# Transposing the heads' results by transfers instead of on TensorE, and taking the last norm's mean off by matmuls

## The chip, the cores and the metric

The kernel runs on one core of one Trainium2 chip. The metric is the time of one execution on the device in microseconds; three plain runs of the kernel before took 1237.16, 1237.46 and 1241.87 us, median 1237.46.

The engines are named as in the profile: PE (TensorE, matmuls; PEld its weight loads), DVE (VectorE), ACT (ScalarE), POOL (GpSimd), SP (SyncE, which issues most transfers). Each runs its own instructions in order and waits on semaphores for the others. SBUF is the memory that all engines and transfers use, PSUM holds the banks that TensorE accumulates into.

## The reference

A decoder trunk of two layers over 256 tokens of width 1024, all in float32. Each layer is

```
x <- LN(alpha*x + 0.5*SwiGLU_1(x))       # width 2816
x <- LN(alpha*x + Mixer(x))
x <- LN(alpha*x + 0.5*SwiGLU_2(x))
```

The mixer projects x to `u, v, q, k, val` and two gates. Branch A norms `gelu(v)`, mixes it over positions by a masked 128x128 matrix in each of 8 channel groups, and multiplies by `gelu(u)`. Branch B is a differential attention with 8 heads: two softmaxes of 64-wide halves of q and k are subtracted, the result is applied to a 128-wide value, and each head's 128 numbers of a token are divided by their root mean square (the part that this change touches):

```
o = a @ v                                    # per head, 256 tokens x 128
o = o * rsqrt(mean(o*o) + eps) * g * (1 - lambda_init)
m = sigmoid(gA) * (h_A @ W_A) + sigmoid(gB) * (h_B @ W_B);  out = m @ W_out
```

## The kernel before

TensorE multiplies in a fast float32 form, and accuracy comes from splitting every operand in a coarse part ("hi") and the rest ("lo"): three products stand for one. Weights are streamed. `stream` loads a piece of 128 x 2048 float32 into one of four "raw" buffers (L154, on SP's queue); ScalarE writes the coarse half pieces `whi` (L167) and VectorE the rest `wlo` (L169) into eight buffers each, so that TensorE works several pieces behind the loads.

Two loops do the large products. `gemm_a2` makes outputs transposed (channels on partitions, the 256 tokens along the row): for each source two blocks of 128 channels, each with eight matmuls of 512 columns (L221, tokens' hi and lo side by side) and eight of 256 (L228). Then ScalarE copies one half of the bank out (L229) and VectorE adds the other (L231), which frees the bank. There are four banks for this, two for a source, so a bank is needed again two sources later. `gemm_b` and `gemm_b2` make outputs with tokens on partitions (L209).

The order of TensorE's instructions is the order in which the program writes them. What is small runs beside the large loops as tasks: a generator is resumed when the count of "beats" (blocks of large matmuls; one source of `gemm_a2` is two beats) has gone on by what it last yielded. On the other engines a scheduler sorts by priority and by what can be ready, and `behind(ins)` puts an instruction after another one of its engine without a wait for it.

In the mixer the sources come as val, then q and k of four head pairs (called hp0 to hp3 here), eight sources of the two gates, v, u, and the two branches. Attention of a head pair is a task (`attend`) that starts when its q and k are there and so runs over the next pairs' projections and over the gates. Its end: TensorE makes `on`, 128 tokens x (2 token halves x 2 heads x 128); ScalarE copies it (L643) and sums squares (L648); GpSimd computes the reciprocal root in fifteen small steps (L651, then `rsqrt4`, L194 to L202); ScalarE rescales `on` (L657); TensorE transposes it in four 128x128 matmuls into a side bank (L662); ScalarE and VectorE split it into `hb` (L667, L668), which the branch reads much later.

The feed-forward part already has a transposition by transfers, for four of its blocks: float32 numbers are seen as pairs of 16-bit words; GpSimd copies them into two planes of words (L498), SP issues one transposing transfer for each plane (L502), and GpSimd joins the planes again (L505).

The norms are made with tokens on partitions. The last one (`last=True`) ends the kernel: statistics in groups (L414, L419), mean off and times g in three pieces (L433), reciprocal root from ScalarE's square root with one Newton step on VectorE (L435 to L437), times root plus b in three pieces (L439), each sent out when ready (L441).

Of the kernel before, what the change touches and what calls it, by code (L numbers as in the profile page):

```python
# [11 lines left out]
F32 = mybir.dt.float32  # L12
# [3 lines left out]
U16 = mybir.dt.uint16  # L16
# [35 lines left out]
def trunk(ctx, tc, x, xT, w13a, w13b, w2, wb, wqk, wa, wbr, wo, gateb, sgug, sgub, sguwT, sgubias, lam, diffg,  # L52
# [89 lines left out]
    latest, added, emptied, silu, turned_by, loaded = [None, None], [None], [None], [None], [None], [None]  # L142
# [5 lines left out]
    def stream(src, width=CH, sub=HC, lent=(), after=(None, None)):  # L148
# [22 lines left out]
        return out  # L171

# [208 lines left out]
    def bc_load(src, after):  # L381
        t = res.tile([P, D], F32, tag="bc", name=name("bc"), bufs=2)
        V.tensor_copy(t[:, :1], after)  # L383
        G.dma_start(t, src.partition_broadcast(P))  # L384
        return t

    class Norm:

# [3 lines left out]
        def __init__(self, l, i, scale, eps, after, last=False):  # L392
# [7 lines left out]
            if last:  # L400
                A.activation(self.g, self.g, AF.Copy, scale=-0.5)
                with behind(silu[0]):
                    A.activation(sm("first", 1), mask[:, :1], AF.Sqrt)
            else:
                self.x = [xs.tile([P, 4, 512], F32R, tag="x", name=name("x")) for _ in range(2)]

        def part(self, t, c, ps):
# [4 lines left out]
            for o in range(s.start, s.stop, self.group):  # L412
                g = o // self.group * 6
                V.bn_stats(out=self.st[t][:, g : g + 6], in_=self.y[t][:, o : o + self.group])  # L414

        def finish(self, t, waits):
# [10 lines left out]
            cuts = (0, 512, 768, D)  # L427
            cuts = [slice(*c) for c in zip(cuts, cuts[1:])]
            ve, sd, r, a = (sm(n, 1) for n in ("ve", "nwy", "nwa", "nwy"))
            V.tensor_scalar(out=ve, in0=mv[:, 1:2], scalar1=self.eps, scalar2=None, op0=ALU.add)  # L430
            A.activation(sd, ve, AF.Sqrt)
            for s in cuts:
# [5 lines left out]
            for n, s in enumerate(cuts):  # L438
                V.scalar_tensor_tensor(out=y[:, s], in0=y[:, s], scalar=r, in1=self.b[:, s],  # L439
                                       op0=ALU.mult, op1=ALU.add)  # L440
                (nc.sync, A)[n % 2].dma_start(out[t * P : (t + 1) * P, s], y[:, s])  # L441
# [37 lines left out]
    def ffn(l, f, i, norm, last=False):  # L479
# [5 lines left out]
        def front(t, ps):  # L485
# [4 lines left out]
            beside(turned(t, p), 0)  # L490

        def turned(t, p):


            pairs = [p[:, n].bitcast(U16).rearrange("p (c w) -> p w c", w=2) for n in range(2)]
            there, back = (p[:, n].bitcast(U16).rearrange("p (w c) -> p w c", w=2) for n in range(2))
            for w in range(2):
                G.tensor_copy(out=there[:, w], in_=pairs[1][:, w])  # L498
            yield 17
            with behind(loaded[0]):  # L500
                for w in range(2):
                    nc.sync.dma_start(back[:, w].rearrange("p (k t) -> p k t", k=4), there[:, w], transpose=True)  # L502
            yield 6
            for w in range(2):
                G.tensor_copy(out=pairs[0][:, w], in_=back[:, w])  # L505
# [33 lines left out]
    def mixer(l, i, norm):  # L539
# [34 lines left out]
        def attend(hp, qT, kT):  # L574
# [83 lines left out]
            yield 0.9  # L658
            b = side_bank()
            for j in range(2):  # L660
                for t in range(NT):
                    PE.transpose(b[:, j * T + t * P : j * T + (t + 1) * P], on[:, (t * 2 + j) * P : (t * 2 + j + 1) * P],  # L662
                                  ident)
            dl = dgs[:, l : l + 1]
            for j in range(2):
                h, s = hb[hp * 2 + j], slice(j * T, (j + 1) * T)
                A.activation(h[:, :T], b[:, s], AF.Copy, scale=dl)  # L667
                V.scalar_tensor_tensor(out=h[:, T:], in0=b[:, s], scalar=dl, in1=h[:, :T].bitcast(F32),  # L668
                                        op0=ALU.mult, op1=ALU.subtract)
# [36 lines left out]
        for h in range(2):  # L706
            s = slice(h * 512, h * 512 + 512)
            G.dma_start(wsT[h], sguwT[l][:, s])
# [142 lines left out]
```

## Time and profile before

| what | value |
|---|---|
| plain runs, median of 3 | 1237.46 us |
| profiled execution | 1238.15 us, span 1236.4 us |
| granted TensorE clock | 0.998 |
| busy: PE / DVE / ACT / POOL | 1226.6 / 883.1 / 754.3 / 133.7 us |
| transposes of the heads' results (L662) | 32 matmuls, 4.8 us busy, first at 272.2, last at 925.7 us |
| transposing transfers (L502) | 16, all in the feed-forward parts |
| attention's end in the first mixer | rescaling of hp0 to hp3 at 271.0, 286.2, 298.9, 311.7 us |
| last large matmul to last output transfer | 1228.0 to 1233.7 us |

A row of the timeline has the start in us, the time it took (for several merged instructions from the first's start to the last's end), the engine, the line in the kernel, the operation, the tiles out<-in, their shape and how many; in brackets the idle time before and what ended it. A row by line gives the shortest, median and longest duration in ns. Idle time of an engine that nothing waits for costs nothing.

### The profile page before, as it was taken

How to read it: one execution, taken by the hardware profiler on the slowest of the kernel's cores; microseconds unless marked ns; L12 is line 12 of the kernel's file. 1: busy time of each engine (PE TensorE's matmuls, PEld its weight loads, DVE VectorE, ACT ScalarE, POOL GpSimd, SP SyncE). 2: the span in 40 equal slices, each digit the busy share in tenths (PEclk: the TensorE clock that was granted, in tenths of full speed). 3: DMA queues.
4: the chain of work that ended last, by engine and by line, in shares of the span. 5: the costliest groups of instructions: out<-in, count | busy, mean ns of one | idle time of the engine just before them, and what ended most of it. 6: DMA issues, size and time to landing. Idle time of an engine off the chain costs nothing.

```text
span 1236.4 us, 17873 instructions
## 1 busy us (share of the span) xinstructions
PE 1226.6 (99%) x6663; PEld 1059.8 (86%) x6663; DVE 883.1 (71%) x1533; ACT 754.3 (61%) x1386; POOL 133.7 (11%) x214
## 2 busy tenths in 40 slices
PE   9999999999999999999999999999999999999997
PEld 8888888888888888888888888888888888888886
DVE  6777567887587987665676765679866879866753
ACT  7676446679665566664466664466885654766640
POOL 1200000244100021000021000002440000210000
PEclk9999999999999999999999999999999999999999
DMA  9965645654754747557547546556456456555540
GB/s 345 265 243 188 222 174 187 223 176 161 257 180 143 244 154 236 180 175 255 195 162 224 186 158 250 204 182 219 168 175 231 151 178 230 196 196 204 177 164 35
DMA packets 49383, 243.97 MB, mean 197 GB/s; under 512 B 14048, under 2 KB 15120, under 8 KB 23184
## 3 DMA queue, kind: packets, MB, share of 16 engines
q1 hardware_dynamic: 45328, 230.18, 54.0%
q0 software_dynamic: 3536, 12.13, 3.3%
q8 instruction: 52, 0.85, 0.3%
q10 hardware_dynamic: 432, 0.52, 0.1%
q14 instruction: 35, 0.29, 0.1%
HBM read 235.47 MB, written 1.05 MB: 191 GB/s over the span
## 4 chain that ended last, share of the span: by engine, by line
PE 97%; ACT 1%; DVE 1%; issue 0%; DMA 0%; SPq 0%; POOL 0%; DVEq 0%; POOLq 0%; ACTq 0%
PE bank L221 37%; PE bank L209 35%; PE bank L228 19%; PE bank L324 2%; PE sbank L588 1%; PE sbank L460 1%; PE sbank L721 1%; PE sbank L640 1%; ACT pp L602 0%; PE sbank L336 0%; PE sbank L638 0%; PE sbank L662 0%; PE sbank L625 0%; DMA swap<-z 0%; DVE qk L568 0%
## 5 line engine op out<-in xcount | busy, mean ns | idle before, releaser
L169 DVE TENSOR_TENSOR wlo<-raw,whi 128x1024 fp32r<-128x1024 f32 (+1 forms) x442 | 498.2, 1145 | 230.8 <-PE bank L228 122.3
L167 ACT ACTIVATE whi<-raw 128x1024 fp32r<-128x1024 f32 (+1 forms) x442 | 425.5, 978 | 280.8 <-PE bank L209 135.3
L221 PE MATMUL bank<-x,whi 128*128 128x512 f32 x1792 | 425.0, 391 | 0.0
L221 PEld LDWEIGHTS bank<-x,whi 128*128 128x128 f32 x1792 | 330.9, 188 | 66.3
L228 PE MATMUL bank<-x,wlo 128*128 128x256 f32 x1792 | 230.9, 284 | 0.0
L228 PEld LDWEIGHTS bank<-x,wlo 128*128 128x128 f32 x1792 | 225.6, 191 | 5.7
L209 PE MATMUL bank<-whi,hhi 128*128 128x512 f32 (+1 forms) x374 | 141.2, 378 | 0.0
L209 PE MATMUL bank<-wlo,hhi 128*128 128x512 f32 (+1 forms) x374 | 141.0, 377 | 0.0
L209 PE MATMUL bank<-whi,hlo 128*128 128x512 f32 (+1 forms) x374 | 140.9, 377 | 0.0
L229 ACT ACTIVATE r<-bank 128x256 f32<-128x256 f32 x256 | 96.6, 379 | 66.4 <-PE bank L228 66.1
L209 PE MATMUL bank<-whi,x 128*128 128x512 f32 x328 | 105.7, 392 | 0.0
L209 PEld LDWEIGHTS bank<-whi,hlo 128*128 128x128 f32 x374 | 70.4, 188 | 13.0
L209 PEld LDWEIGHTS bank<-wlo,hhi 128*128 128x128 f32 x374 | 70.4, 188 | 12.7
L209 PEld LDWEIGHTS bank<-whi,hhi 128*128 128x128 f32 x374 | 70.4, 188 | 12.7
L209 PEld LDWEIGHTS bank<-whi,x 128*128 128x128 f32 x328 | 61.6, 188 | 12.6
L209 PE MATMUL bank<-wlo,x 128*128 128x512 f32 x164 | 63.9, 390 | 0.0
L384 POOL DMA_DIRECT2D bc<-in_lng x6 | 3.2, 534 | 480.2 <-DVE bc L383 480.2
L466 ACT ACTIVATE xf<-sbank,ln_b,ln_g 128x128 f32<-128x128 f32 x80 | 30.1, 457 | 40.1 <-PE sbank L460 40.1
L231 DVE TENSOR_TENSOR silu<-bank,r 128x256 f32<-128x256 f32 x144 | 54.2, 416 | 0.5 <-ACT r L229 0.5
L564 POOL TENSOR_TENSOR swap<-swap,sin_t 128x512 f32<-128x512 f32 x16 | 26.6, 1664 | 244.1 <-DMA swap<-z 239.3
L410 DVE SCALAR_TENSOR_TENSOR xtok<-xtok,bank 128x512 f32<-128x512 f32 (+1 forms) x25 | 16.5, 662 | 42.7 <-PE bank L209 42.7
L498 POOL COPY planes<-planes 128x512 uint16<-128x512 uint16 x16 | 27.1, 1718 | 177.4 <-DVE planes L489 177.4
(174 smaller groups left out, 1295.6 us busy)
## 6 DMA issues: line engine op xcount, KB each, us to landing
raw<-in_w13a SPq DMA_DIRECT2D x72, 1024.0 KB, 5.0
raw<-in_w SPq DMA_DIRECT2D x40, 1024.0 KB, 4.9
raw<-in_wa SPq DMA_DIRECT2D x24, 1024.0 KB, 6.0
raw<-in_wb SPq DMA_DIRECT2D x16, 1024.0 KB, 5.0
raw<-in_wqk SPq DMA_DIRECT2D x16, 1024.0 KB, 5.2
raw<-in_wbr SPq DMA_DIRECT2D x16, 1024.0 KB, 4.9
raw<-in_w13b SPq DMA_DIRECT2D x12, 1024.0 KB, 5.1
raw<-in_wo SPq DMA_DIRECT2D x8, 1024.0 KB, 5.0
```

The costliest lines, as they stand in the source:

```text
L167: A.activation(h, r, AF.Copy)
L169: V.tensor_tensor(out=w, in0=r, in1=h.bitcast(F32), op=ALU.subtract)
L209: PE.matmul(ps, xx, w, start=start and n == 0, stop=stop and n == 2)
L221: PE.matmul(b[-1], hi[:, k * P : (k + 1) * P], xc(k), start=k == 0, stop=False)
L228: PE.matmul(b[n][:, :T], lo[:, k * P : (k + 1) * P], xc(k)[:, :T], start=False, stop=k == KT - 1)
L229: emptied[0] = A.activation(r[:, s], b[n][:, T:], AF.Copy, scale=scale).ins
L231: a = V.tensor_tensor(out=z[:, s], in0=b[n][:, :T], in1=r[:, s], op=ALU.add)
L324: PE.matmul(ps[t][m], x[:, j, o + t * P : o + (t + 1) * P], y, start=k0 + j == 0 and o == 0 and y is hi, stop=k0 + j == KT - 1 and y is lo)
L410: V.scalar_tensor_tensor(out=self.y[t][:, s], in0=self.y[t][:, s], scalar=self.scale, in1=ps, op0=ALU.mult, op1=ALU.add)
L466: A.activation(xf[:, s], b[:, s], AF.Identity, scale=self.gT[:, f], bias=self.bT[:, f])
L498: G.tensor_copy(out=there[:, w], in_=pairs[1][:, w])
L564: turned_by[0] = G.tensor_tensor(out=s3, in0=s3, in1=s, op=ALU.mult).ins
```

## The change

Three edits.

1. The transposition by transfers becomes a function, `transposed`, and the heads' results use it too: GpSimd makes the planes in a new buffer `moved`, SP transposes them into `on`, GpSimd joins them in `moved`, and the split into `hb` reads `moved`. The waits between are counted in beats: 1 after the rescaling, 10 before the transfers are placed in SP's queue, then 0.3 and 0.3. The 32 TensorE transposes are gone. The split instructions are placed behind the last emptying of a bank.
2. In the last norm the second token half's first 768 columns are multiplied by g as soon as their statistics are taken. For two of the three pieces TensorE then adds, in a side bank, identity times y and a diagonal of minus the mean times g; ScalarE makes that diagonal from the negative identity. The pieces go in the opposite order, the small ones first. Variance plus epsilon is made on GpSimd, and ScalarE's square root takes epsilon as its bias from the raw variance.
3. The spatial weights' load on GpSimd's queue is placed behind the latest broadcast load (`spread`).

```diff
+    def transposed(src, out, via, first, second):
+        def planes(v):
+            return v.bitcast(U16).rearrange("p (w c) -> p w c", w=2)
+        def numbers(v):
+            return v.bitcast(U16).rearrange("p (c w) -> p w c", w=2)
+        for w in range(2):
+            G.tensor_copy(out=planes(out)[:, w], in_=numbers(src)[:, w])
+        yield first
+        with behind(loaded[0]):
+            for w in range(2):
+                nc.sync.dma_start(planes(via)[:, w].rearrange("p (k t) -> p k t", k=4), planes(out)[:, w],
+                                  transpose=True)
+        yield second
+        for w in range(2):
+            G.tensor_copy(out=numbers(out)[:, w], in_=planes(via)[:, w])
...
-        G.dma_start(t, src.partition_broadcast(P))
+        spread[0] = G.dma_start(t, src.partition_broadcast(P)).ins
...
+                self.minus = s512("minus")
+                A.activation(self.minus[:, :P], ident, AF.Copy, scale=-1.0)
...
+            if self.last and t == NT - 1 and s.stop < D:
+                V.tensor_tensor(out=self.y[t][:, s], in0=self.y[t][:, s], in1=self.g[:, s], op=ALU.mult)
...
-            V.tensor_scalar(out=ve, in0=mv[:, 1:2], scalar1=self.eps, scalar2=None, op0=ALU.add)
-            A.activation(sd, ve, AF.Sqrt)
-            for s in cuts:
+            G.tensor_scalar(out=ve, in0=mv[:, 1:2], scalar1=self.eps, scalar2=None, op0=ALU.add)
+            A.activation(sd, mv[:, 1:2], AF.Sqrt, bias=self.eps_t)
+            rows = [y[:, s] for s in cuts]
+            if t == NT - 1:
+                rows[1:] = [side_bank()[:, : s.stop - s.start] for s in cuts[1:]]
+                for b, s in zip(rows[1:], cuts[1:]):
+                    PE.matmul(b, ident, y[:, s], start=True, stop=False)
+                diag = self.minus[:, P : 2 * P]
+                A.activation(diag, self.minus[:, :P], AF.Copy, scale=mv[:, 0:1])
+                for b, s in zip(rows[1:], cuts[1:]):
+                    PE.matmul(b, diag, self.g[:, s], start=False, stop=True)
+            for s in cuts[: 1 if t == NT - 1 else 3]:
...
-            yield 0.9
-            b = side_bank()
-            for j in range(2):
-                for t in range(NT):
-                    PE.transpose(b[:, j * T + t * P : j * T + (t + 1) * P], on[:, (t * 2 + j) * P : (t * 2 + j + 1) * P],
-                                  ident)
+            yield 1
+            moved = slots("moved", 2)[0]
+            yield from transposed(on, moved, on, 10, 0.3)
+            yield 0.3
...
+                with behind(emptied[0]):
+                    A.activation(hi, f, AF.Copy, scale=dl)
+                with behind(added[0]):
+                    V.scalar_tensor_tensor(out=lo, in0=f, scalar=dl, in1=hi.bitcast(F32), op0=ALU.mult,
+                                            op1=ALU.subtract)
...
-            G.dma_start(wsT[h], sguwT[l][:, s])
+            with behind(spread[0]):
+                G.dma_start(wsT[h], sguwT[l][:, s])
```

The order on GpSimd in the first mixer, at the start of hp2's root (`ss` is its sum of squares; `ve`, `yi`, `nwa`, `nwy` its steps). Lines are those of each kernel: L651 and L194 to L202 before are L675 and L215 to L223 now. Before:

```order
L202 TENSOR_TENSOR nwy_2860<-nwa_2859,nwy_2854 128x4
L651 TENSOR_TENSOR ss_2984<-s_564_2985,ss_2984 128x4
L194 TENSOR_SCALAR ve_3053<-ss_2984 128x4
L195 TENSOR_SCALAR yi_3054<-ve_3053 128x4
L199 TENSOR_TENSOR nwa_3057<-yi_3054 128x4
L200 TENSOR_TENSOR nwa_3057<-nwa_3057,ve_3053 128x4
L201 TENSOR_SCALAR nwa_3057<-nwa_3057 128x4
L202 TENSOR_TENSOR nwy_3058<-nwa_3057,yi_3054 128x4
```

And now, where L184 are copies there and L192 copies back, `moved_2812` is hp0's and `moved_3016` hp1's:

```order
L223 TENSOR_TENSOR nwy_2854<-nwa_2853,nwy_2848 128x4
L192 COPY moved_2812<-on_2552 128x512 x2
L184 COPY moved_3016<-on_2772 128x512 x2
L675 TENSOR_TENSOR ss_2978<-s_564_2979,ss_2978 128x4
L215 TENSOR_SCALAR ve_3041<-ss_2978 128x4
L216 TENSOR_SCALAR yi_3042<-ve_3041 128x4
L220 TENSOR_TENSOR nwa_3045<-yi_3042 128x4
L221 TENSOR_TENSOR nwa_3045<-nwa_3045,ve_3041 128x4
L192 COPY moved_3016<-on_2772 128x512
L222 TENSOR_SCALAR nwa_3045<-nwa_3045 128x4
L192 COPY moved_3016<-on_2772 128x512
L223 TENSOR_TENSOR nwy_3046<-nwa_3045,yi_3042 128x4
```

Six copies have come in, two of them inside the root's steps; hp0's copies there stand earlier, inside hp1's root, six small steps before its end.

The order on ScalarE around the rescaling of hp2 (`on_2982` before, `on_2976` now; `r<-bank` empties a bank). Before:

```order
L229 ACTIVATE r_3131<-bank_3113 128x256
L657 ACTIVATE on_2982<-on_2982,nwy_3070 128x128 x4
L643 ACTIVATE on_3154<-sbank_3147 128x512
L684 ACTIVATE gate_3099<-gz_3132,gbh 128x256
L648 ACTIVATE sbank_3147,ss_3156<-sbank_3147 128x128
L229 ACTIVATE r_3131<-bank_3122 128x256
L648 ACTIVATE sbank_3147,ss_3156<-sbank_3147 128x128 x3
L684 ACTIVATE gate_3099<-gz_3132,gbh 128x256
L167 ACTIVATE whi_3418<-raw_3416 128x1024
L667 ACTIVATE hb_2048<-sbank_3194,dgs 128x256
L667 ACTIVATE hb_2049<-sbank_3194,dgs 128x256
```

And now:

```order
L250 ACTIVATE r_3119<-bank_3101 128x256
L681 ACTIVATE on_2976<-on_2976,nwy_3058 128x128 x4
L667 ACTIVATE on_3142<-sbank_3135 128x512
L709 ACTIVATE gate_3087<-gz_3120,gbh 128x256
L672 ACTIVATE sbank_3135,ss_3144<-sbank_3135 128x128
L250 ACTIVATE r_3119<-bank_3110 128x256
L672 ACTIVATE sbank_3135,ss_3144<-sbank_3135 128x128 x3
L709 ACTIVATE gate_3087<-gz_3120,gbh 128x256
L167 ACTIVATE whi_3410<-raw_3408 128x1024
L167 ACTIVATE whi_3414<-raw_3408 128x1024
```

The rescaling and the emptying of the bank behind it have kept their places; the two splits into `hb` have left.

SP's queue at the same time, from v's first weights on. Before:

```order
L154 DMA raw_3382<-in_wb 128x2048
L154 DMA raw_3416<-in_wb 128x2048
L154 DMA raw_3456<-in_wb 128x2048
L154 DMA raw_3490<-in_wb 128x2048
L154 DMA raw_3597<-in_wa 128x2048
```

And now, with `on_2552`, `on_2772` and `on_2976` of hp0, hp1 and hp2:

```order
L154 DMA raw_3366<-in_wb 128x2048
L188 DMA_TRANSPOSE on_2552<-moved_2812 128x4x128 x2
L154 DMA raw_3408<-in_wb 128x2048
L188 DMA_TRANSPOSE on_2772<-moved_3016 128x4x128 x2
L154 DMA raw_3448<-in_wb 128x2048
L154 DMA raw_3490<-in_wb 128x2048
L188 DMA_TRANSPOSE on_2976<-moved_3182 128x4x128 x2
L154 DMA raw_3597<-in_wa 128x2048
```

A pair of transposing transfers now stands between the loads, each waiting for its copies there.

More of the change, by code (lines that the diff above doesn't have):

```diff
@@ L140, in finish_tasks @@
                 turn(task)
-    latest, added, emptied, silu, turned_by, loaded = [None, None], [None], [None], [None], [None], [None]
+    latest, added, emptied, silu, turned_by, loaded, spread = [None, None], [None], [None], [None], [None], [None], [None]
     def behind(ins):
@@ L426, in finish @@
                 return
-            cuts = (0, 512, 768, D)
-            cuts = [slice(*c) for c in zip(cuts, cuts[1:])]
+            cuts = [slice(*c) for c in ((768, D), (512, 768), (0, 512))]
             ve, sd, r, a = (sm(n, 1) for n in ("ve", "nwy", "nwa", "nwy"))
-            V.tensor_scalar(out=ve, in0=mv[:, 1:2], scalar1=self.eps, scalar2=None, op0=ALU.add)
-            A.activation(sd, ve, AF.Sqrt)
-            for s in cuts:
+            G.tensor_scalar(out=ve, in0=mv[:, 1:2], scalar1=self.eps, scalar2=None, op0=ALU.add)
[10 more added lines that the diff above has]
+            for s in cuts[: 1 if t == NT - 1 else 3]:
                 V.scalar_tensor_tensor(out=y[:, s], in0=y[:, s], scalar=mv[:, 0:1], in1=self.g[:, s],
@@ L437, in finish @@
             V.tensor_scalar(out=r, in0=a, scalar1=3.0, scalar2=r, op0=ALU.subtract, op1=ALU.mult)
-            for n, s in enumerate(cuts):
-                V.scalar_tensor_tensor(out=y[:, s], in0=y[:, s], scalar=r, in1=self.b[:, s],
-                                       op0=ALU.mult, op1=ALU.add)
+            for n, (s, v) in enumerate(zip(cuts, rows)):
+                V.scalar_tensor_tensor(out=y[:, s], in0=v, scalar=r, in1=self.b[:, s], op0=ALU.mult, op1=ALU.add)
                 (nc.sync, A)[n % 2].dma_start(out[t * P : (t + 1) * P, s], y[:, s])
@@ L489, in front, with turned @@
             V.tensor_tensor(out=s, in0=s, in1=ps[1], op=ALU.mult)
[L490 to L505, printed above, removed]
+            beside(turned(t, s, p), 0)
+        def turned(t, s, p):
+            yield from transposed(s, p[:, 0], p[:, 1], 17, 6)
             x = p[:, 0].rearrange("p (k t) -> p k t", k=4)
@@ L657, in attend @@
                     A.activation(on[:, s], on[:, s], AF.Copy, scale=r[:, q : q + 1])
-            yield 0.9
-            b = side_bank()
-            for j in range(2):
-                for t in range(NT):
-                    PE.transpose(b[:, j * T + t * P : j * T + (t + 1) * P], on[:, (t * 2 + j) * P : (t * 2 + j + 1) * P],
-                                  ident)
+            yield 1
+            moved = slots("moved", 2)[0]
+            yield from transposed(on, moved, on, 10, 0.3)
+            yield 0.3
             dl = dgs[:, l : l + 1]
             for j in range(2):
[L666 to L669, printed above, removed]
+                hi, lo = (hb[hp * 2 + j][:, o : o + T].rearrange("p (t c) -> p t c", t=NT) for o in (0, T))
+                f = moved.rearrange("p (t j c) -> p j t c", t=NT, j=2)[:, j]
+                with behind(emptied[0]):
[3 more added lines that the diff above has]
+                                            op1=ALU.subtract)
         for hp in range(HEADS // 2):
```

2 lines of the change are left out of this document (added).

## The prediction

> **What bounds the kernel now.** I read the page's busy times and chain first, then the PE timeline around the transposes that go, then GpSimd, ScalarE and VectorE in the first mixer's gate stage, then the last ten microseconds.
>
> ```profile
> PE 1226.6 (99%) x6663; PEld 1059.8 (86%) x6663; DVE 883.1 (71%) x1533; ACT 754.3 (61%) x1386; POOL 133.7 (11%) x214
> PE 97%; ACT 1%; DVE 1%; issue 0%; DMA 0%; SPq 0%; POOL 0%; DVEq 0%; POOLq 0%; ACTq 0%
> ```
>
> TensorE is the bound from end to end: 97% of the chain. A TensorE instruction removed is time won, a new wait on TensorE is time lost, and everything else counts only through TensorE or in the tail after its last matmul. The profiled execution took 1238.15 us (span 1236.4 and 1.75 around it); the three plain runs have their median 0.69 lower, at 1237.46. I sum against 1238.15 and take 0.69 off at the end.
>
> **Removed: 32 TensorE transposes.** Two pairs of sources of the second gate, the first pair's start without transposes, the other with four in its middle:
>
> ```profile
> 306.51 3.82 PE L221 MATMUL bank<-x,whi 128*128 128x512 f32 x16
> 310.17 2.08 PE L228 MATMUL bank<-x,wlo 128*128 128x256 f32 x16
> ...
> 312.08 2.01 PE L221 MATMUL bank<-x,whi 128*128 128x512 f32 x8
> 313.93 0.60 PE L662 MATMUL sbank<-ident,on 128*128 128x128 f32 x4
> 314.28 2.10 PE L221 MATMUL bank<-x,whi 128*128 128x512 f32 x8
> 316.22 2.07 PE L228 MATMUL bank<-x,wlo 128*128 128x256 f32 x16
> L662 PE MATMUL sbank<-ident,on x32: 270/272/307, 272.2 to 925.7; 128*128 128x128 f32 x32
> ```
>
> From the first L221 to the first L228 it is 310.17 - 306.51 = 3.66 us without transposes and 316.22 - 312.08 = 4.14 with four: 0.48 for a head pair. Eight head pairs (32 / 4) free 8 x 0.48 = 3.84 us. The 272 ns are the length of one, overlapped with the next; priced by them, 32 x 0.272 = 8.7 us would go, which the starts rule out unless the pipeline refills differently.
>
> The Trainium skill (TensorE: Matmul & The Clock Gate, Part 4: PE-mode transpose) gives about 275 ns for a transpose within a kernel, which as an estimate is 8.8 us for 32; the length in the row agrees, the spacing does not, and the spacing decides here.
>
> **Added on GpSimd: 32 copies, and a new place in its queue.** Per head pair two copies "there", two transposing transfers on SP, two copies "back". The same helper exists in the feed-forward part, so its rows are the prices:
>
> ```profile
> L498 POOL COPY planes<-planes x16: 612/1576/4890, 26.0 to 1070.8; 128x512 uint16<-128x512 uint16 x16
> 463.56 3.03 SPq L502 DMA_TRANSPOSE planes<-planes  x2
> 470.12 2.74 POOL L505 COPY planes<-planes 128x512 uint16<-128x512 uint16 x2 [9.22 <-DMA planes<-planes]
> 471.70 2.52 SPq L502 DMA_TRANSPOSE planes<-planes  x2
> 477.82 2.00 POOL L505 COPY planes<-planes 128x512 uint16<-128x512 uint16 x2 [4.96 <-DMA planes<-planes]
> ```
>
> "There" costs 2 x 1.576 = 3.15 us a pair, from the first issue to the first copy back 6.56 or 6.12 (I take 6.4), "back" 2.74 or 2.00 (2.3). None of that is on TensorE. But GpSimd runs in order, and it also computes the heads' reciprocal roots (rsqrt4, fifteen small steps), which ScalarE needs to rescale each head pair. In the new order hp1's copies back sit inside hp2's root, five steps in, with nine to follow (one step lies between the copies). So hp2's root waits for hp1's transfer, which waits for hp1's copies there, which stand behind hp0's copies back. The chain starts inside hp1's root, at the step of the first row here:
>
> ```profile
> 278.17 0.20 POOL L200 TENSOR_TENSOR nwa<-nwa,ve 128x4 f32<-128x4 f32 x1
> 296.37 0.20 POOL L199 TENSOR_TENSOR nwa<-nwy 128x4 f32<-128x4 f32 x1
> 297.25 0.20 POOL L202 TENSOR_TENSOR nwy<-nwa,nwy 128x4 f32<-128x4 f32 x1
> 298.61 0.36 ACT L229 ACTIVATE r<-bank 128x256 f32<-128x256 f32 x1
> 298.87 1.27 ACT L657 ACTIVATE on<-on,nwy 128x128 f32<-128x128 f32 x4
> 301.21 0.37 ACT L229 ACTIVATE r<-bank 128x256 f32<-128x256 f32 x1
> 301.81 0.42 DVE L231 TENSOR_TENSOR gz<-bank,r 128x256 f32<-128x256 f32 x1
> ```
>
> hp0 there 278.4 + 3.15 = 281.5; transfer to 287.9; back to 290.2; hp1 there to 293.4; transfer to 299.8; back with the step between (2.3 + 0.3) to 302.4; nine steps at (297.25 - 296.37) / 3 = 0.29 to **305.0**. The old kernel rescaled hp2 at 298.87. ScalarE now stands there some 6 us, and queued behind the rescaling is L229 of the block before (301.21), then VectorE's L231, which empties the bank that TensorE reuses two sources on. From the rescaling's start to that bank's release is 301.81 + 0.42 - 298.87 = 3.36, so the bank is free at 308.4. TensorE reached it at the ninth of the L221 that began at 306.51, about 308.3; three head pairs freed by then move that to 306.9. **New stall: 1.5 us.** The next bank is needed 312.08 - 308.3 = 3.8 us after this one, and what ScalarE has in its queue between the two releases is about as long, so I add no second stall; a microsecond there lies inside the range.
>
> So a mixer wins 4 x 0.48 = 1.92 and loses 1.5: 0.42. I take the second mixer as the first: **0.85 for both**. Bounds of the stall: with copies there at 0.612 the root is ready before 301, and nothing is lost; with a pair of 5.45 (the longest, below) in place of both pairs there it is ready at 309.6, and 6.1 us are lost per mixer.
>
> **Moved to SP.** Sixteen transfers stand between weight loads, and hp2's hold the load behind them:
>
> ```profile
> 301.97 19.22 SPq L154 DMA_DIRECT2D raw<-in_wa  x4
> 321.07 1.06 ACT L167 ACTIVATE whi<-raw 128x1024 fp32r<-128x1024 f32 x1 [0.81 <-PE bank L209]
> ```
>
> That load, issued at 301.97, would go at 305.0 + 1.3 (rescaling) + 3.15 + 2.5 (two issues) = 312. Its split comes at 321.07, after a wait for TensorE and not for the load; even at the 6.56 us of the slower pair above it lands by 318.6. Cost nothing; cover 2.5 us, and behind that the pieces already split that TensorE has still to use.
>
> The spatial weights' load now follows the broadcast of the gate norm on GpSimd:
>
> ```profile
> 328.33 0.56 POOL L384 DMA_DIRECT2D bc<-in_sgug  x1 [11.41 <-DVE bc L383]
> 354.68 1.05 PE L721 MATMUL sbank<-wsT,vg 128*128 128x128 f32 x8
> ```
>
> hp3's copies end near 330 by the same sum, so the weights go at about 331, 23 us ahead of their first use. Nothing. The heads' splits (L667, L668) leave the attention stage for the v and u stages, same count, same sizes: nothing, and less crowding where they were.
>
> **The tail.** VectorE's six passes after the last matmul become four, and TensorE takes the mean off two pieces:
>
> ```profile
> 1227.97 0.28 PE L209 MATMUL bank<-whi,hlo 128*128 128x256 f32 x1
> 1229.21 0.26 DVE L419 BATCH_NORM_AGGREGATE mv<-st 128x2 f32<-128x24 f32 x1
> 1229.58 1.53 DVE L433 SCALAR_TENSOR_TENSOR xtok<-xtok,mv,bc 128x512 f32<-128x512 f32 x3
> 1229.75 0.20 ACT L431 ACTIVATE nwy<-ve 128x1 f32<-128x1 f32 x1 [9.33 <-DVE ve L430]
> 1231.03 0.15 DVE L435 RECIPROCAL nwa<-nwy 128x1 f32<-128x1 f32 x1
> 1231.22 0.27 DVE L436 TENSOR_SCALAR nwy<-nwa,ve 128x1 f32<-128x1 f32 x1
> 1231.53 0.21 DVE L437 TENSOR_SCALAR nwa<-nwy,nwa 128x1 f32<-128x1 f32 x1
> 1231.78 1.54 DVE L439 SCALAR_TENSOR_TENSOR xtok<-xtok,nwa,bc 128x512 f32<-128x512 f32 x3
> 1232.56 1.12 SPq L441 DMA_DIRECT2D out_x<-xtok  x2
> 298.18 0.39 PE L638 MATMUL sbank<-val,aT 128*128 128x128 f32 x2
> 298.40 0.61 PE L640 MATMUL sbank<-val,aT 128*128 128x128 f32 x4
> 298.85 0.39 PE L638 MATMUL sbank<-val,aT 128*128 128x128 f32 x2
> ```
>
> A float32 product of 128 columns takes two matmuls; three products took 298.85 - 298.18 = 0.67, so 0.22 each, 0.45 for 256 columns and 0.9 for 512. Identity times y runs from 1228.1 to 1229.4, hidden behind the statistics. The mean is ready at 1229.47. Square root 0.2, diagonal of L657's size (four overlapped take 1.27, so one alone about 0.4, an estimate): 1230.1. TensorE's second round: 256 columns to 1230.9, 512 to 1231.75, a drain of 0.61 - 4 x 0.11 = 0.17 included. VectorE: one piece of 256 (a quarter of L433, 0.38) to 1229.9, reciprocal and two steps to 1230.6, a quarter of L439 to 1231.0, the 256 from PSUM to 1231.4, then a wait of 0.35 for TensorE and the 512 (0.75) to 1232.55. The old last transfer was issued at about 1233.34 (1232.56 + 1.12 - 0.34). **Win 0.8**; 1.15 without that wait, 0.3 if the diagonal comes half a microsecond later. The second variance-plus-epsilon on GpSimd costs 0.2 and is needed at 1230.0; hidden by the piece of 256.
>
> **Sum.** 1238.15 - 0.85 - 0.8 = 1236.5 for a profiled execution; less 0.69, **1235.8 us**.
>
> **Rivals.**
>
> - *No stall* (0.27). VectorE idles more in the gate stage than where the copies were priced, so copies there may take near 0.612, and the root is ready before 303.5. Against it: the copies stand beside VectorE's splits. Then 3.84 + 0.8 = 4.6 go: 1232.8.
> - *The stall outgrows the win: slower* (0.20). GpSimd's copies wait for VectorE, and the other way round:
>
> ```profile
> 641.46 5.45 POOL L498 COPY planes<-planes 128x512 uint16<-128x512 uint16 x2 [7.48 <-DVE planes L489]
> 273.32 1.29 POOL L564 TENSOR_TENSOR swap<-swap,sin_t 128x512 f32<-128x512 f32 x1 [2.32 <-DMA swap<-z]
> 273.78 1.91 DVE L169 TENSOR_TENSOR wlo<-raw,whi 128x1024 fp32r<-128x1024 f32 x1 [1.16 <-ACT whi L167]
> ```
>
>   One pair of 5.45 in place of 3.15 puts the root at 307.3, the stall at 3.8 per mixer: 7.6 against 4.6, 1237.46 + 3.0 = 1240.5. It decides from a stall of 2.3, a root at 305.8, only 0.8 after my estimate. The Trainium skill (SBUF — State Buffer, SBUF: two separate sides) says that VectorE and GpSimd hold a shared port pair exclusively for a whole instruction; by it every copy beside a two-input VectorE operation is held like this, and the two rows above agree.
> - *The transposes free their whole length* (0.02), 8.7 + 0.8: 1228.0. It is the price by the length above; the spacing speaks against it.
> - *The transfers starve the splits, or the diagonal is late* (0.06): some 1 to 3 us given back, 1237 to 1239.
>
> **How the numbers follow.** My case has 0.45, and its own range, with the root between 303.5 and 305.8, is 1232.8 to 1237.5. To hold 8 in 10 I go from 1232.3 (no stall, tail at its best) to 1240.6 (one long pair per mixer). Half a percent, about what a measurement here tells from no change, is 6.2 us. Faster than 1231.3 needs the whole lengths or unseen slack: 0.05. Slower than 1243.6 needs two long pairs per mixer: 0.08. Else the same: 0.87.
>
> **What would show it.** Right: no transposes of heads on TensorE; four gaps' worth of 0.48 gone per mixer; in the second gate a ScalarE rescaling of hp2 that waits several microseconds for GpSimd's root, and a TensorE gap of 1 to 2 us at the third source behind it; last output transfer issued about 4.6 us after the last large matmul's start in place of 5.4. Wrong: GpSimd's root of hp2 ready before 303 on the old scale (no gap, 1233), or TensorE gaps at other places: the v stage's first banks, L721, or a load.

## The result, and the profile after

The changed kernel takes 1231.23 us (median of six runs, 1230.87 to 1232.84) beside 1237.74 for the kernel before on the same chip: a ratio of 0.9945, with a 95% interval of 0.9931 to 0.9959. That is 6.5 us gained, where 1.65 were forecast (4.6 by the rival without a stall). The profiled execution took 1231.87 us, its span 1230.2 against 1236.4 before. In the changed kernel L242, L249 and L252 are before's L221, L228 and L231, L612 and L651 are before's L588 and L627, and L184, L188 and L192 the three steps of the transposing helper.

Busy times and chain of the page after:

```profile
PE 1224.3 (100%) x6639; PEld 1057.5 (86%) x6639; DVE 890.9 (72%) x1532; ACT 755.3 (61%) x1388; POOL 161.2 (13%) x248
PE 99%; DMA 0%; DVE 0%; ACT 0%; issue 0%; ACTq 0%
```

GpSimd has 27.5 us more work, and TensorE's share of the chain went from 97% to 99%. The bound is still TensorE, so the time must have left its stream or the tail. The same matmuls stand in both traces in the same order, so each one's start can be subtracted. Of the 6.28 us between the two profiled executions, 5.57 are gone when the last large matmul starts. They go in steps: eight at the places of the transposes (3.84 together, 0.48 each), one of 1.24 and one of 0.72 us at two places where nothing was transposed, less a start-up that came 0.23 later. The last large matmul starts at 1227.97 before and at 1222.40 after.

The two unforeseen steps are at the score matmuls of the last head pair in each mixer. First TensorE's timeline of the kernel before there (start, length, instruction, and in brackets the idle time ahead and what ended it):

```profile
278.93 0.70 PE L588 MATMUL sbank<-qk,qk 64*128 64x256 f32 x2
280.18 1.57 PE L588 MATMUL sbank<-qk,qk 64*128 64x256 f32 x14 [0.56 <-ACT aT L627]
...
890.96 2.29 PE L588 MATMUL sbank<-qk,qk 64*128 64x256 f32 x16
```

and the same of the kernel after:

```profile
278.68 1.58 PE L612 MATMUL sbank<-qk,qk 64*128 64x256 f32 x16
...
887.49 1.58 PE L612 MATMUL sbank<-qk,qk 64*128 64x256 f32 x16
```

Sixteen score matmuls take 1.58 us for every head pair after. Before, the last head pair's took 281.75 - 278.93 = 2.82 in the first mixer and 2.29 in the second: two matmuls ran, then TensorE stood until ScalarE had copied aT out of a small bank. (The expectations below count from the start of the large matmul ahead to that of the second one behind: 2.16 us for a free group, 3.4 and 2.9 for these two.) What ScalarE did there, before:

```profile
277.60 0.45 ACT L667 ACTIVATE hb<-sbank,dgs 128x256 fp32r<-128x256 f32 x1
...
278.91 0.46 ACT L667 ACTIVATE hb<-sbank,dgs 128x256 fp32r<-128x256 f32 x1
...
279.53 0.60 ACT L627 ACTIVATE aT<-sbank 128x512 f32<-128x512 f32 x1
```

The first head pair's old step is in the middle of it. Its two halves of hb (L667) stand ahead of the copy aT on ScalarE, and they are read from one of the four small banks, which so stays taken while the scores ask for banks. In the kernel after there is no hb at this place, and the copy aT runs at 278.39.

The stall that I forecast is not there. ScalarE's and TensorE's timelines of the kernel after in the second gate:

```profile
300.00 1.28 ACT L681 ACTIVATE on<-on,nwy 128x128 f32<-128x128 f32 x4 [2.10 <-POOL nwy L223]
...
304.05 3.82 PE L242 MATMUL bank<-x,whi 128*128 128x512 f32 x16
```

hp2's root was ready at 299.97 and not at 305.0; ScalarE waited 2.10 us for it, which reaches nobody: the sixteen L242 go without a break. GpSimd's queue shows why. The begin of hp2's root in the kernel before:

```profile
291.22 0.28 POOL L651 TENSOR_TENSOR ss<-s,ss 128x4 f32<-128x4 f32 x1 [9.27 <-ACT sbank L648]
```

and the queue of the kernel after, from hp0's copies on:

```profile
278.90 2.20 POOL L184 COPY moved<-on 128x512 uint16<-128x512 uint16 x2
284.98 1.46 POOL L192 COPY moved<-on 128x512 uint16<-128x512 uint16 x2 [2.25 <-DMA on<-moved]
287.02 1.36 POOL L184 COPY moved<-on 128x512 uint16<-128x512 uint16 x2 [0.59 <-ACT on L681]
290.68 0.27 POOL L675 TENSOR_TENSOR ss<-s,ss 128x4 f32<-128x4 f32 x1 [2.29 <-ACT sbank L672]
...
293.07 0.77 POOL L192 COPY moved<-on 128x512 uint16<-128x512 uint16 x1
...
294.89 0.76 POOL L192 COPY moved<-on 128x512 uint16<-128x512 uint16 x1
...
298.95 1.02 POOL L223 TENSOR_TENSOR nwy<-nwa,nwy 128x4 f32<-128x4 f32 x1
301.35 1.16 POOL L184 COPY moved<-on 128x512 uint16<-128x512 uint16 x2 [1.38 <-ACT on L681]
```

A pair there took 2.20, 1.36 and 1.16 us where I had 3.15, and hp0's copies back began 3.84 us after their transfers' issue (SP issued them at 281.14) where I had 6.4. So the chain of copies and transfers was over in time: hp2's root began at 290.68, when ScalarE's squares came, as it had at 291.22 before, where GpSimd had been idle for 9.27 us; and hp1's copies back, at 293.07 and 294.89, had no wait for their transfer. They only made the root longer: 9.29 us to 299.97, where it had taken 6.23 (291.22 to 297.45), half of the difference for the two copies and the rest for small steps, of which four took over 1 us where two had before (most take 0.2).

The tail after, from VectorE's, ScalarE's, TensorE's and SP's timelines:

```profile
1223.64 0.26 DVE L448 BATCH_NORM_AGGREGATE mv<-st 128x2 f32<-128x24 f32 x1
1224.20 0.39 ACT L466 ACTIVATE minus<-minus,mv 128x128 f32<-128x128 f32 x1
1224.64 1.56 PE L468 MATMUL sbank<-bc,minus 128*128 128x256 f32 x4 [0.66 <-ACT minus L466]
1226.23 0.75 DVE L476 SCALAR_TENSOR_TENSOR xtok<-sbank,nwa,bc 128x512 f32<-128x512 f32 x1 [0.17 <-PE sbank L468]
1225.70 1.65 SPq L477 DMA_DIRECT2D out_x<-xtok  x2
```

The last transfer is issued at 1225.70 + 1.65 - 0.34 = 1227.01, 4.61 us after the last large matmul's start, where it was 5.37: 0.76 gained.

### The profile page after: what moved, and what is told of

Same layout as the page of the kernel before. It is cut to its first block, busy times and chain, and to the rows that moved or that the text cites. A ratio compares the mean times of both kernels' runs of the same rounds, so it can differ in the third digit from the quotient of the medians.

```text
span 1230.2 us, 17916 instructions
## 1 busy us (share of the span) xinstructions
PE 1224.3 (100%) x6639; PEld 1057.5 (86%) x6639; DVE 890.9 (72%) x1532; ACT 755.3 (61%) x1388; POOL 161.2 (13%) x248
## 3 DMA queue, kind: packets, MB, share of 16 engines
HBM read 235.47 MB, written 1.05 MB: 192 GB/s over the span
## 4 chain that ended last, share of the span: by engine, by line
PE 99%; DMA 0%; DVE 0%; ACT 0%; issue 0%; ACTq 0%
PE bank L242 38%; PE bank L230 36%; PE bank L249 20%; PE bank L345 2%; PE sbank L612 1%; PE sbank L496 1%; PE sbank L664 1%; PE sbank L747 1%; PE sbank L662 0%; DMA xraw<-in_xT 0%; PE sbank L649 0%; PE sbank L654 0%; PE sbank L468 0%; DVE xtok L476 0%; ACT whi L195 0%; DVE st L441 0%
## 5 line engine op out<-in xcount | busy, mean ns | idle before, releaser
L242 PE MATMUL bank<-x,whi 128*128 128x512 f32 x1792 | 422.7, 391 | 0.0
L242 PEld LDWEIGHTS bank<-x,whi 128*128 128x128 f32 x1792 | 331.5, 188 | 66.7
L249 PE MATMUL bank<-x,wlo 128*128 128x256 f32 x1792 | 231.0, 284 | 0.0
L249 PEld LDWEIGHTS bank<-x,wlo 128*128 128x128 f32 x1792 | 225.6, 191 | 5.6
L588 POOL TENSOR_TENSOR swap<-swap,sin_t 128x512 f32<-128x512 f32 x16 | 26.5, 1655 | 243.2 <-DMA swap<-z 133.3
L252 DVE TENSOR_TENSOR silu<-bank,r 128x256 f32<-128x256 f32 x144 | 54.2, 417 | 0.0
L184 POOL COPY planes<-planes 128x512 uint16<-128x512 uint16 x16 | 26.1, 1659 | 178.9 <-DVE planes L525 178.9
```

The source lines that it names most:

```text
L184: G.tensor_copy(out=planes(out)[:, w], in_=numbers(src)[:, w])
L242: PE.matmul(b[-1], hi[:, k * P : (k + 1) * P], xc(k), start=k == 0, stop=False)
L249: PE.matmul(b[n][:, :T], lo[:, k * P : (k + 1) * P], xc(k)[:, :T], start=False, stop=k == KT - 1)
L252: a = V.tensor_tensor(out=z[:, s], in0=b[n][:, :T], in1=r[:, s], op=ALU.add)
L588: turned_by[0] = G.tensor_tensor(out=s3, in0=s3, in1=s, op=ALU.mult).ins
```

## The experiments

Two theories stood against each other at first. **A**: the gain is the transposes' 3.8 us, the score waits of the last head pair, which the old step caused (1.96 in this pair of traces), and 0.76 in the tail. **B**: the score waits went for another reason.

### Each half alone

Only the transfers (with the later wsT loads), the last norm as before:

```diff
  (the changed kernel)
-    the last norm's piece products on TensorE, diagonal by ScalarE
+    the last norm as in the kernel before
```

> Before with the head transposes by transfers and the later wsT loads; the last norm is left as it was. Theory A (the gain is 3.86 us of transposes and 1.96 us of waits of the last head pair's score matmuls, both on TensorE, and 0.76 us behind its last matmul): TensorE's last large matmul stands 5.8 us earlier than before's, all eight groups of score matmuls take 2.16 us, and the last transfer is issued 5.4 us after that matmul; about 1232.0 us where before takes 1237.7. Rival B (the score waits were an accident of where the work fell, and return when the tail's code is taken out, since nothing in the change was aimed at them): 3.9 us earlier, about 1233.9 us.

Measured: 1231.99 us against 1237.7, ratio 0.9958 (0.9944 to 0.9973). The last large matmul starts at 1221.72, 6.25 earlier than before's; 0.47 of that stands already at the 40th matmul, so 5.8 are the step's. All eight groups of scores take 2.16 us with their neighbours, and the last transfer is issued 5.37 us after the last large matmul. As A has it.

Only the tail:

```diff
  (the kernel before)
-    the last norm as it was
+    the last norm's piece products on TensorE, diagonal by ScalarE
```

> Before with the last norm's edit alone; the heads' results still go through TensorE. Theory A: TensorE's matmuls up to the last large one stand where before's stand within 0.2 us, the score matmuls of the last head pair again take 3.4 and 2.9 us, and the last transfer is issued 4.6 us after the last large matmul instead of 5.4: about 1237.0 us, 0.76 below before. Rival B (the tail's edit also moves the rest, and some of the 1.96 us of score waits belongs to it): 1235 to 1236 us.

Measured: 1236.6 us against 1237.7, ratio 0.9987 (0.9975 to 1.0). The last transfer is issued 4.61 us after the last large matmul: 0.76 again. But that matmul stands 1.20 us earlier than in the trace of before, and the tail's edit cannot be why: 0.46 is there by the 40th matmul, and the other 0.75 at the first mixer's last scores, whose groups TensorE's timeline shows as

```profile
278.45 2.08 PE L603 MATMUL sbank<-qk,qk 64*128 64x256 f32 x16
889.71 2.31 PE L603 MATMUL sbank<-qk,qk 64*128 64x256 f32 x16
```

Against the free 1.58 that is a wait of 0.50 in the first mixer where the profiled execution of before had 1.24, and of 0.73 in the second, where it had 0.72. So the first mixer's wait differs by some 0.7 us between executions of the same instructions up to there, and the 1.96 of my accounting is 1.2 here. The two halves' medians lie 5.7 and 1.1 us below before's, 6.8 together, beside 6.5 for the whole change: they add up within the intervals.

### What made the scores wait

The old step kept beside the new one, in the changed kernel:

```diff
-            yield 1
+            yield 0.9
+            b = side_bank()
+            ... four PE.transpose of on into b, as before
+            for j in range(2):
+                A.activation(h[:, :T], b[:, s], AF.Copy, scale=dl)
+                V.scalar_tensor_tensor(out=h[:, T:], in0=b[:, s], scalar=dl, in1=h[:, :T].bitcast(F32), ...)
+            yield 0.1
             moved = slots("moved", 2)[0]
```

> The changed kernel with before's step kept beside the new one: TensorE's four transposes per head pair into a small bank, and the two halves of hb read from it, at the old place; the new step then writes hb again with the same numbers. Theory A (the score waits come from that step): TensorE loses 3.86 us to the 32 transposes and 1.96 us to the last head pair's score matmuls, which take 3.4 and 2.9 us again: about 1237.0 us. Rival B (the waits go with something else in the change): 3.9 us, about 1235.1 us, all groups of score matmuls at 2.16 us. More than 1237.5 us would be the new step and the old one in each other's way.

Measured: 1236.61 us, ratio to before 0.9991 (0.9981 to 1.0). TensorE's timeline at the last scores of both mixers:

```profile
278.33 2.19 PE L612 MATMUL sbank<-qk,qk 64*128 64x256 f32 x16
890.15 2.33 PE L612 MATMUL sbank<-qk,qk 64*128 64x256 f32 x16
```

The waits are back, 0.61 and 0.75 us. With nothing taken out, the old step alone puts the time back to 0.7 us below before's, and the tail, which stays changed, is worth 0.76. So the waits come with the step, not with something else in the change; B falls. Inside the step there are two candidates: ScalarE's work, and the bank.

ScalarE's work without the bank:

```diff
-            yield 1
+            yield 0.9
+            for j in range(2):
+                A.activation(hb[hp * 2 + j][:, :T], mask[:, :T], AF.Copy, scale=dgs[:, l : l + 1])
+            yield 0.1
```

> The changed kernel with two activations of 128x256 per head pair on ScalarE at the place where the old step made hb's halves; they read the mask and not a bank, so the order of the small banks stays that of the changed kernel. Theory S2 (the score waits come from ScalarE alone: hb's halves of 0.45 us stand ahead of the copies aT that free the banks): the copies end about 1.1 us later, and the last head pair's score matmuls wait 0.5 to 1.25 us in the first mixer and 0 to 0.7 in the second: 1231.7 to 1233.2 us. Theory S1 (they come from the bank: the transposes' bank is held until hb's second half is read, so that the scores' second bank is the one that the copy aT must empty first): no wait, all groups at 2.16 us, 1231.2 us.

Measured: 1232.11 us, ratio to before 0.9957 (0.9942 to 0.9971). The first mixer's last group takes 1.75 us, the second's 1.58:

```profile
278.63 1.75 PE L612 MATMUL sbank<-qk,qk 64*128 64x256 f32 x16
```

That is a wait of 0.18 us in one mixer: less than S2 had at the least (0.5), more than S1's nothing; the time, which lies within S2's range, is too close to the changed kernel's to decide. ScalarE's work alone does not bring the waits back.

A bank taken, but read early:

```diff
-            yield 1
+            yield 0.9
+            b = side_bank()
+            PE.transpose(b[:, :P], ident, ident)
+            for j in range(2):
+                V.tensor_copy(hb[hp * 2 + j][:, :P], b[:, :P])
+            yield 0.1
```

> The changed kernel with one small bank more taken per head pair at the old place: a single TensorE transpose of the identity into it, and two VectorE copies of 128 columns that read it and stand well ahead of the last head pair's scores; nothing more on ScalarE. Theory S3 (the score waits need a bank that stays held: the old step's bank was read last by VectorE behind ScalarE's second half of hb): a bank that is read early leaves all groups of score matmuls at 2.16 us, and the eight transposes cost 0.1 to 0.25 us each, 0.8 to 2 us: 1232 to 1233.2 us. Theory S4 (taking a fifth bank in the round is enough by itself, however early it is read): waits of 0.3 to 1.2 us at the last head pair's scores in each mixer on top of that, 1233 to 1235.5 us.

Measured: 1232.99 us, ratio to before 0.9966 (0.9953 to 0.9979). All groups take 1.58 us, and the last large matmul stands 1.14 us later than in the changed kernel: 0.14 for each of the eight transposes. One bank more in the round costs no wait when it is read early, as S3 has it. So neither part does it alone; the old step as a whole does.

How the two parts work together can be read from the packed traces. They do not name the banks, but they record which engine each of the scores' four banks is waited for at its first weight load. With the old step in its old place (before, only the tail, the old step kept) it is ScalarE, ScalarE, ScalarE and VectorE, in both mixers. In the changed kernel the first waits for nobody and the other three for ScalarE. With the bank that is read early it is ScalarE, VectorE, ScalarE and ScalarE. Since the scores of the head pair ahead the old order has taken four banks: for hp1's `on`, for the transposes, and two for aT; only the transposes' is read last by VectorE, the others by ScalarE. So, as far as these waits tell, the transposes' bank, held until hb's second half is read, is given out last, and the first aT bank comes second instead of third. The scores need the second bank 0.1 us after they begin and the third 0.75 us after.

The copy that empties this aT bank ended 1.20 us after the scores' begin in before's first mixer (279.53 + 0.60 against 278.93), behind hb's halves on ScalarE, 0.72 with ScalarE's extra work, and 0.30 in the changed kernel. At 0.72 the third place does not wait and the second would; the 0.18 us of that run are a wait for the other aT copy. In all six groups with the old step in its old place the waiting weight load starts 0.05 us after the aT copy's end. So the wait is S1's order of the banks and S2's late copy together.

The old step moved, with all transposes kept; in the kernel before:

```diff
-            yield 0.9
+            yield 4
             b = side_bank()
```

> Before with one number changed: the TensorE transposes of a head pair's result come 4 beats later instead of 0.9, so that the first head pair's stand behind the last head pair's scores and not ahead of them. All 32 transposes stay. Theory A (the 1.96 us are a matter of where the first head pair's step falls, not of how the transposing is done): all groups of score matmuls take 2.16 us and the kernel gains 1.96 us: about 1235.8 us. Rival B (the last head pair's scores wait for their banks anyway, because the gates load ScalarE and VectorE from there on): 1237.7 us.

Measured: 1236.3 us against 1237.35, ratio 0.9993 (0.9983 to 1.0003). The scores take 1.58 us in the first mixer and 1.65 in the second:

```profile
278.40 1.58 PE L588 MATMUL sbank<-qk,qk 64*128 64x256 f32 x16
...
282.81 0.60 PE L662 MATMUL sbank<-ident,on 128*128 128x128 f32 x4
...
889.35 1.65 PE L588 MATMUL sbank<-qk,qk 64*128 64x256 f32 x16
```

The last large matmul starts at 1226.09, 1.89 before that of the kernel before. By the time alone (1.05 us between medians, and an interval that reaches past 1) this could not be told from no change; the timeline tells it. So the waits were a matter of where the first head pair's step fell in the program, and one number takes nearly all of them away without a transfer.

### The stall that was forecast

GpSimd's copies there repeated for the second head pair, so that hp2's root comes later; five times over, and ten:

```diff
-        for w in range(2):
-            G.tensor_copy(out=planes(out)[:, w], in_=numbers(src)[:, w])
+        for w in range(2 * times):
+            G.tensor_copy(out=planes(out)[:, w % 2], in_=numbers(src)[:, w % 2])
```

> The changed kernel, in which GpSimd makes the copies ahead of the transfer five times over for the second head pair of each mixer (8 copies more of 0.6 to 0.8 us each, up to 1.6 where a weight split of VectorE runs beside one). The third head pair's root stands behind them on GpSimd. Theory A (the forecast stall is a real mechanism whose price was wrong: it begins once that root is ready later than 303.5 us in the profiled time of before): the root moves from 300.0 to 299 to 302 us, which is still short of it, and TensorE does not wait: 1231.2 us as the changed kernel. Rival B (the point from which it decides is earlier, since ScalarE's rescale already waited 2.1 us for the root): 0.5 to 2 us more in each mixer.

> The same with ten times over (18 copies more, 12 to 15 us of GpSimd in each mixer). Theory A: the third head pair's root is ready at 305 to 309 us, past 303.5, and TensorE waits for a bank in the gates for what it is past that point: 1.5 to 5.5 us per mixer, 1234 to 1242 us. Rival C (a late root does not reach TensorE at all, since ScalarE has other work to turn to or the banks last longer than I counted): no wait of TensorE in the gates, 1231 to 1232 us.

Measured with five: 1232.19 us, ratio to before 0.9955 (0.9939 to 0.9971), and no gap in the gates, so B falls. ScalarE and TensorE:

```profile
302.52 1.28 ACT L681 ACTIVATE on<-on,nwy 128x128 f32<-128x128 f32 x4 [4.66 <-POOL nwy L223]
...
304.28 3.82 PE L242 MATMUL bank<-x,whi 128*128 128x512 f32 x16
```

Measured with ten: 1246.54 us, ratio to before 1.0074 (1.0054 to 1.0094); GpSimd, ScalarE, then TensorE:

```profile
307.41 0.20 POOL L223 TENSOR_TENSOR nwy<-nwa,nwy 128x4 f32<-128x4 f32 x1
...
307.64 1.28 ACT L681 ACTIVATE on<-on,nwy 128x128 f32<-128x128 f32 x4 [10.31 <-POOL nwy L223]
...
303.75 2.00 PE L242 MATMUL bank<-x,whi 128*128 128x512 f32 x8
310.86 3.78 PE L242 MATMUL bank<-x,whi 128*128 128x512 f32 x8 [5.11 <-DVE gz L252]
...
927.86 3.49 PE L242 MATMUL bank<-x,whi 128*128 128x512 f32 x8 [5.31 <-DVE gz L252]
```

The way from a late root to TensorE is real and at the forecast place: the ninth matmul of that L242 waits for VectorE to empty the bank. From the root to the bank it is 310.86 - 307.61 = 3.25 us (3.36 in my sum). The gap of 5.11 puts the deciding point at a root of 307.61 - 5.11 = 302.5; the kernel with five times over has its root at 302.48 and no gap, and the changed kernel with 299.97 is 2.5 us short of it. Rival C falls. A has the mechanism but not the sizes: the point was off by one microsecond, as the scores' 1.24 us bring TensorE there earlier, and the time lies past its 1242, because a gap costs more than its length (see the last section). In both runs hp1's copies back stand behind hp2's root on GpSimd, so they test a late root and not a late transfer.

### The later load of wsT

```diff
-            with behind(spread[0]):
-                G.dma_start(wsT[h], sguwT[l][:, s])
+            G.dma_start(wsT[h], sguwT[l][:, s])
```

> The changed kernel without the hold on the loads of wsT (the third edit). Theory A (the edit is worth nothing by itself; the loads have 20 us of room): 1231.2 us, TensorE's matmuls as in the changed kernel within 0.2 us. Rival B (the loads then stand on GpSimd's queue ahead of the last head pair's copies back, which wait behind them, and hb is late for the outputs): 1232 to 1234 us, with a wait of TensorE in the last gate or at the outputs.

Measured: 1233.55 us (1231.83 to 1239.6), ratio to before 0.9975 (0.9957 to 0.9993). The copies back of the last head pair are not late, so B's mechanism falls, and its time was met by luck. But A falls too: the last large matmul stands 1.46 us later than in the changed kernel, although the matmuls ahead stood 0.36 earlier; 1.8 us are lost, in the first mixer, at a place that neither theory named. GpSimd, then TensorE, of this kernel:

```profile
332.06 0.64 POOL L734 TENSOR_SCALAR_AFFINE_SELECT wsT<-wsT 128x512 f32<-128x512 f32 x1 [4.61 <-DMA wsT<-in_sguwT]
332.64 0.56 POOL L405 DMA_DIRECT2D bc<-in_sgug  x1
...
350.16 2.08 PE L242 MATMUL bank<-x,whi 128*128 128x512 f32 x8 [0.38 <-DVE u L252]
...
353.30 0.94 PE L746 MATMUL sbank<-wsT,vg 128*128 128x128 f32 x6 [0.84 <-DVE vg L728]
```

and the same load of the changed kernel:

```profile
325.39 0.64 POOL L405 DMA_DIRECT2D bc<-in_sgug  x1 [2.95 <-DVE bc L404]
```

Without the hold GpSimd waits for wsT's loads ahead of its two masking passes, and the gate norm's broadcast goes out 7.25 us later (332.64 against 325.39). VectorE then finishes vg late, and TensorE's first spatial matmuls wait. In the kernel before, GpSimd was through with wsT by 316.9 and idle until 328.33, so no hold was needed there. The hold is a repair for what the copies do to GpSimd's queue, worth 1.8 us of TensorE in this trace. The loss need not come in every execution: two of the six runs, 1231.83 and 1231.92 us, are as fast as the changed kernel.

### A shorter end

The last piece of the tail in two halves, with the two queues of the output transfers exchanged so that the last one stays on SP's:

```diff
-            cuts = [slice(*c) for c in ((768, D), (512, 768), (0, 512))]
+            cuts = [slice(*c) for c in ((768, D), (512, 768), (256, 512), (0, 256))]
...
-            for s in cuts[: 1 if t == NT - 1 else 3]:
+            for s in cuts[: 1 if t == NT - 1 else 4]:
...
-                (nc.sync, A)[n % 2].dma_start(out[t * P : (t + 1) * P, s], y[:, s])
+                (A, nc.sync)[n % 2].dma_start(out[t * P : (t + 1) * P, s], y[:, s])
```

> The changed kernel with the last norm's piece of 512 columns cut in two pieces of 256, so that the last pass of VectorE and the last transfer are half as long, and TensorE's last product is 0.45 us shorter than the one before it ends. Theory A (behind the last matmul the chain is TensorE's products and then VectorE's last pass of 0.75 us): the last pass of 256 takes about 0.4, and the last transfer is issued 0.2 to 0.4 us sooner after the last large matmul: 1230.9 us, within what can be told from no change. Rival B (one transfer and one pass more cost their fixed part, 0.6 us for an issue and some 0.1 us for a pass): 1231.3 to 1231.6 us.

Measured: 1231.17 us, ratio to before 0.9951 (0.9934 to 0.9967), the changed kernel's 0.9945 again. In the trace the last transfer is issued 4.45 us after the last large matmul in place of 4.61, and the span ends 7.27 after it in place of 7.76. A gain of 0.16 at the issue is less than A's least, and in the time it cannot be told from nothing.

## Why the prediction was wrong, point by point

It was wrong: 1231.23 us lies under the range's low end of 1232.3, and just past the bound for "faster" (1231.3), to which I gave 0.05.

- **TensorE bounds the kernel from end to end.** Right: 99% of the chain after.
- **Thirty-two transposes at 0.48 per head pair, 3.84 us.** Right: eight steps between the traces, 3.84 together. The rival that priced them by their length (8.7) is wrong.
- **New stall of 1.5 us per mixer, 3.0 in all.** Wrong, the first failed step and the larger one: nothing was lost. What failed is the chain through hp0's copies, hp1's copies and hp1's transfer. I priced it so high that it ended last and put hp2's root at 305.0; the root came at 299.97. The chain was done before the root needed it, what set the root's begin was ScalarE's squares (290.68), and the 9.27 us that GpSimd had been idle ahead of this root took the copies in. The leg behind the root is confirmed to a tenth of a microsecond (3.36 against 3.25 from root to bank). As for the prices, I took the copies and transfers from the feed-forward part: there a copy took 1.58 us in the median, here 0.84 in the mean, and hp0's transfers took 3.84 us from issue to the copies back in place of 6.4. The rival "no stall" had named the copies' reason. The transfers' is open: in the feed-forward part of this same trace a 1 MB load is issued 0.42 us ahead of the pair that took 6.3 us (468.34 and 468.76), and ahead of hp0's the last one goes 5.96 us earlier (275.18), but no run changed the load alone.
- **The heads' splits leave the attention stage: "nothing, and less crowding where they were".** Wrong, the second failed step: smaller than the first, but it took the time out of the range. The crowding was costing TensorE 1.96 us in the profiled execution (1.2 and 1.4 in two others with the same step): the row with 0.56 of idle time behind "ACT aT L627" stood in the trace of before, and I did not ask what else was waiting on the step that goes. This term is in no case and no rival of mine; the range's low end of 1232.3 was no stall and the tail at its best.
- **SP's loads held by the transfers: nothing.** Right: no wait of TensorE for a weight load appears.
- **The load of wsT moved: nothing.** Right for the kernel as changed, and it hides that the same copies can cost 1.8 us without it.
- **The tail, 0.8.** Right: 0.76, with the wait of VectorE for TensorE at 0.17 in place of 0.35.
- **Slower, from a stall that outgrows the win.** Wrong here, but possible: with 18 copies more per mixer the kernel took 1246.54.

With the two failed steps put right, 1238.15 - 3.84 - 1.96 - 0.76 = 1231.6 against 1231.87 profiled, and 0.23 of what is between is the later start-up.

## What to carry to other kernels

When a step leaves the bounding engine, look not only at its own instructions but at every wait near it that ends in its neighbours' queues or in the buffers it held; such a wait goes with it, and sometimes one number that moves the step is enough. A duration is the price of an instruction among its neighbours there: the same copy took twice as long, in the mean, where VectorE's splits were denser. Before a chain is added up, look for the idle time that it can run in. When a root's or a load's lateness is in dispute, compute the point from which it decides and test on both sides of that point.

## What the runs showed of the hardware

**A GpSimd copy that begins during a VectorE weight split ends about half a microsecond after the split.** Groups of GpSimd's instructions in the kernel after (last columns: busy us, mean ns), then the VectorE split beside one of its copies:

```profile
L184 POOL COPY planes<-planes 128x512 uint16<-128x512 uint16 x16 | 26.1, 1659 | 178.9 <-DVE planes L525 178.9
L184 POOL COPY moved<-on 128x512 uint16<-128x512 uint16 x16 | 13.0, 839 | 3.9 <-ACT on L681 3.9
...
278.87 1.22 DVE L169 TENSOR_TENSOR wlo<-raw,whi 128x1024 fp32r<-128x1024 f32 x1
```

The copy that began at 278.90, 0.03 us after this split, took 1.65 us and so ended 0.46 after it; the next, at 280.50 beside VectorE's passes over the score banks, took 0.60, and the two at 301.35, with VectorE idle, 0.61 each. The same instruction has the two prices, and how many of them begin during a split sets the mean: of the sixteen copies here three took 1.65 to 1.70 us and thirteen 0.60 to 0.78 (mean 0.84); of the sixteen in the feed-forward part fourteen took 1.48 or more (mean 1.66). The Trainium skill (SBUF — State Buffer, SBUF: two separate sides) says that the two engines hold a port pair exclusively for a whole instruction; the trace agrees for the splits.

**After a gap of 5 us TensorE ran at half its clock, for some 5.5 us after one gap and 3 us after another.** A table by stages of the kernel with ten times over (columns: stretch, its length, busy us of PE, PEld, DVE, ACT and POOL with counts, granted clock, DMA share, GB/s):

```profile
310.80:314.80 4.00, 3.94 (x10) 3.17 (x11) 2.00 (x5) 3.75 (x10) 3.34 (x11) 0.50 0.52 98
314.80:316.30 1.50, 1.50 (x9) 1.50 (x8) 1.11 (x1) 1.50 (x4) 1.39 (x2) 0.50 0.98 415
316.50:320.00 3.50, 3.50 (x20) 3.01 (x19) 3.46 (x5) 3.22 (x9) 3.17 (x7) 1.00 0.95 346
927.90:930.70 2.80, 2.80 (x7) 2.22 (x8) 0.90 (x1) 2.77 (x8) 2.38 (x7) 0.50 0.42 94
```

The gaps ended at 310.86 and 927.86. Behind both, the matmuls of 512 columns start 0.43 us apart in place of 0.23. Against the changed kernel TensorE loses 7.9 us there for a gap of 5.1, and 7.0 for one of 5.3 in the second mixer. My price for the slower rival took a gap at its length.
